# A hybrid decoder block in fp32: finer loads in the prologue, later spreading products, and three S5 inputs on GpSimd's DMA queue

## The chip, the cores and the metric

The kernel runs on one core of a Trainium2 chip. A core has a matrix engine (TensorE, PE in the profile; its weight loads are PEld), VectorE (DVE), ScalarE (ACT), GpSimd (POOL) and SyncE (SP), which here only issues DMAs. TensorE writes into PSUM banks, everything else works in SBUF; data comes from and goes to device memory (DRAM) by 16 DMA engines. A DMA is issued by SyncE, ScalarE or GpSimd, each with a queue of its own (q1, q10 and q0 in the profile). The metric is the time of one execution in device microseconds, as a median over runs; lower is better.

## The reference

One layer of a decoder block over 512 tokens and 16 meta tokens, width 1024, all in fp32. Cut to what matters here:

```
h    = concat(meta, x)                      # 528 x 1024
xn   = rmsnorm(h, g_mix_pre)
proj = xn @ w_in                            # q, k, v, r, a_low, u, z_gla, z_ssm
y_gla = gated linear attention(q, k, v, a_low, r) @ w_o_gla
y_ssm = glu(gelu(s5(u; a, log_step, b, c, d)) @ w_glu)
h    = h + rmsnorm((sigmoid(z_gla) * y_gla + sigmoid(z_ssm) * y_ssm) @ w_out, g)
h    = h + rmsnorm(relu(rmsnorm(h, g) @ w_ff1)**2 @ w_ff2, g)
```

The change touches the start: the norm of x, the first products xn @ w_in for the columns of u, and the loading of the S5 parameters b and c.

## The kernel before, in words

**Products in split precision.** Every fp32 operand is split into a high part (a rounding by ScalarE) and a low part (the rest, by VectorE), and a product of two is made of three matmuls: high-high, high-low, low-high (`mm3`, lines 190 to 198). A weight is taken as column tiles of 128: 1024 rows make eight row tiles of 128 (KT = 8), so a column tile is 512 KB and a product with it takes 8 x 3 matmuls. The tokens are handled in two parts, 256 and 272 wide (HALVES): x's first 256 tokens, then the other 256 with the 16 meta tokens.

**The prologue (lines 455 to 684)** starts the work on u before the norm of x is known. It takes x transposed (`xT`), scales its rows by the gain g alone, splits that (`rh`, `rl`, by `taken_raw`, lines 526 to 530) and multiplies the first five column tiles of the u weights with it ("raw products"); the missing factor, one per token, is applied when the product leaves PSUM (`u_took`). The factors come from x in its row layout: `squared` (ScalarE) sums the squares of a tile of 128 tokens, `rooted` (ScalarE and VectorE) makes the inverse root, `spread` (lines 550 to 556) turns the column of factors into rows by small matmuls against the identity, and `rows_of` copies them out of PSUM on ScalarE. Tokens 0 to 255 have spread(0), the others spread(1).

The order in the text, pinned on TensorE, VectorE and ScalarE:

- lines 603 to 609: for each row tile k, x's row tile is scaled and split, and between them the first two weights w0 and w1 are split in parts: row tiles 0-1, 2-3 and 4-7;
- lines 610 to 615: the products of w0 and w1 side by side, first for the first tokens (48 matmuls), then, after eight more `taken_raw`, for the others (48);
- lines 616 to 634: w2 is split, three x tiles are squared, the first two rooted; the raw product of w2 for the first tokens, with spread(0) put in ahead of row tile 3; then VectorE takes the two finished products out, scales x (`scaled`, four row tiles), splits w3, scales two more, roots the rest;
- lines 637 to 659: w2 for the other tokens, w3 for the first with spread(1) ahead of its row tile 3, w3, w4 and w4 for the rest, while x, now normed, is split into `xh` and `xl`;
- lines 660 on: the small weight of a_low (`wa`) is split; `low_rank` (line 698) is the first product with the normed x.

**Loads.** A few go by ScalarE's queue first. Two lists of SyncE loads follow (lines 475 to 480 and 495 to 514). In both, `behind()` ties each issue behind the one before it (`tc.issue_after`), so the order is the written one. The second list loads the rest of x transposed in two halves, a's parameters, weight 2, x in rows (four tiles and the meta tokens), weights 3 and 4, small weights, weight 5, then c in two layouts and b (`CA`, `CB`, `BA`, 512 KB each), weights 6 and 7. Weight tiles rotate through three buffers (`raw_w`, line 166), so a load from the fourth on waits until an earlier tile is split.

**GpSimd's queue** has in this stretch the load of `vecs` (line 515), the stores of the u tiles (`u_out`, line 285) and, at lines 681 to 683, a store of the norm factors to DRAM (`rsd`) and two loads of them in another layout (`s0`). Instructions that are not pinned or tied are ordered by the framework's scheduler, engine by engine.

`CA` is first read by `c_rows` (line 870), `BA` at line 932, `CB` in `Block.tables` (line 1174).

Of the kernel before, what the change touches and what calls it, by code (L numbers as in the profile page):

```python
# [19 lines left out]
KT = D // P  # L20
# [30 lines left out]
def hybrid_block(ctx: ExitStack, tc: tile.TileContext, io, out: bass.AP):  # L51
    nc = tc.nc
# [28 lines left out]
    def mk(pool, shape, dt=F32, tag=None, **kw):  # L81
        count[0] += 1
        name = f"{tag or 'x'}_{count[0]}"
        size = 1
        for n in shape[1:]:
            size *= n
        if pool not in lined or size % LINE == 0:
            return pool.tile(shape, dt, tag=tag or name, name=name, **kw)
        t = pool.tile([shape[0], -(-size // LINE) * LINE], dt, tag=tag or name, name=name, **kw)[:, :size]
        if len(shape) == 2:  # L90
            return t
        dims = " ".join("abcd"[: len(shape) - 1])
        return t.rearrange(f"p ({dims}) -> p {dims}", **dict(zip("abcd", shape[1:])))

    def f32(t):
        return t.bitcast(F32)
# [35 lines left out]
    def bank(tag="sm"):  # L132
        return mk(ps_mm if tag == "mm" else ps_sm, [P, 512], tag=tag)
# [29 lines left out]
    def split_hi(dst, src, scale=1.0):  # L163
        return S.activation(dst, src, AF.Copy, scale=scale)  # L164

    def raw_w(src):

        kt, n = src.shape[0] // P, src.shape[1]
        raw = mk(wp, [P, kt, P], tag="wraw", bufs=3)
        return nc.sync.dma_start(raw[:, :, :n], src.rearrange("(k p) n -> p k n", p=P)), raw  # L170

    def split_w_hi(raw):
        hi = mk(wp, [P, raw.shape[1], P], F32R, tag="whi", bufs=3)
        split_hi(hi, raw)
        return hi
# [6 lines left out]
    def split_w(raw):  # L182
        hi = split_w_hi(raw)
        return hi, split_w_lo(raw, hi)
# [15 lines left out]
    def feat_tile(w, xh, xl, c0, c1, ps, m=P, kt=KT, within=None):  # L200
        hi, lo = w
        return mm3(ps, lambda k: hi[:, k, :m], lambda k: lo[:, k, :m], lambda k: xh[:, k, c0:c1], lambda k: xl[:, k, c0:c1], kt, within)
# [90 lines left out]
    CA = mk(p5, [P, GRP, HG], tag="CA")  # L293
    CB = mk(p5, [P, GRP, HG], tag="CB")
    BA = mk(p5, [P, GRP, HG], tag="BA")
# [9 lines left out]
    def scratch():  # L305
        return mk(pg, [P, TT, P], tag="sc0", bufs=1)
# [154 lines left out]
    xT = mk(pxt, [P, KT, NT], tag="xT")  # L461
    rh, rl = (mk(pxt, [P, KT, LINE + SEQ], F32R, tag=t)[:, :, :NT] for t in ("rh", "rl"))
    raws, xts, loaded = [mk(wp, [P, KT, P], tag="wraw", bufs=3) for _ in range(2)], {}, None

    def behind():
        return tc.issue_after(loaded.ins) if loaded else ExitStack()

    def first_w(queue, i, k, n):
        return queue.dma_start(raws[i][:, k : k + n], w_in[k * P : (k + n) * P, C_U + i * P : C_U + (i + 1) * P].rearrange("(k p) n -> p k n", p=P))
# [2 lines left out]
    held = first_w(nc.scalar, 1, 0, 2)  # L472
    with tc.issue_after(held.ins):
        S.activation(warm, warm, AF.Sqrt)
    for i, k, n in (("x", 0, 1), ("x", 1, 1), (0, 2, 2), ("x", 2, 2), (1, 2, 2), ("x", 4, 2), (0, 4, 4), (1, 4, 4), ("x", 6, 2)):
        with behind():
            if i == "x":
                loaded = nc.sync.dma_start(xT[:, k : k + n, :256], io["x_cols0"][:, k : k + n])
            else:
                loaded = first_w(nc.sync, i, k, n)  # L480
# [7 lines left out]
    def x_load(t):  # L488
        n = NM if t == TT else P
        xt = mk(pxt, [P, D], tag="xt", bufs=5)  # L490
        xts[t] = xt, n
        return nc.sync.dma_start(xt[:n], io["meta_tokens"] if t == TT else io["x"][0, t * P : (t + 1) * P, :])

    early = []
    for kind, i in (("h", 0), ("h", 4), ("a", 0), ("u", 2), ("x", 0), ("x", 1), ("x", 2), ("x", 3), ("x", 4), ("u", 3), ("u", 4), ("w", 0), ("g", 0), ("u", 5), ("c", 0), ("u", 6), ("u", 7)):
        with behind():
            if kind == "x":
                loaded = x_load(i)
            elif kind == "h":
                loaded = nc.sync.dma_start(xT[:, i : i + 4, 256:], io["x_cols1"][:, i : i + 4])  # L500
            elif kind == "a":
                loaded = nc.sync.dma_start(ab, io["a_step"])
            elif kind == "w":
                wraw = mk(pg, [P, KT, 16], tag="waraw")
                loaded = nc.sync.dma_start(wraw, w_in[:, C_A : C_A + 16].rearrange("(k p) n -> p k n", p=P))
            elif kind == "g":
                wgu = scratch()[:96].rearrange("p a b -> p (a b)")
                loaded = nc.sync.dma_start(wgu, io["w_gates"])
            elif kind == "c":
                for dst, src in ((CA, io["c_cols"][0]), (CB, io["c_cols"][1]), (BA, io["b_cols"][0])):  # L510
                    loaded = nc.sync.dma_start(dst.rearrange("p g h -> p (g h)"), src)
            else:
                loaded, raw = raw_w(w_in[:, C_U + i * P : C_U + (i + 1) * P])
                raws.append(raw)
# [11 lines left out]
    def taken_raw(k, q):  # L526

        g, cols = g8[:, k : k + 1], slice(*HALVES[q])
        S.activation(rh[:, k, cols], xT[:, k, cols], AF.Copy, scale=g)
        V.scalar_tensor_tensor(rl[:, k, cols], xT[:, k, cols], g, f32(rh)[:, k, cols], op0=ALU.mult, op1=ALU.subtract)  # L530
# [19 lines left out]
    def spread(q):  # L550

        ps = bank()
        for j, i in enumerate(range(3 * q, 3 * q + 2) if not q else range(2, TT + 1)):
            n = xts[i][1]
            PE.matmul(ps[:, j * P : j * P + n], rs[:n, i : i + 1].to_broadcast([n, P]), ident[:n, :n], start=True, stop=True)
        return ps

    def rows_of(q, ps):
        a, b = HALVES[q]
        S.copy(rows[:, a:b], ps[:, : b - a])  # L560
        src = ps.rearrange("p (c s) -> p s c", s=T8)
        S.copy(rowp[:, :, 2 + a // T8 : 34 + a // T8], src[:, :, :32])
        if q:
            S.copy(rowp[:, :, :2], src[:, :, 32:34])
# [14 lines left out]
    def low(q, ks):  # L579
        cols, to = quarters_of(q)  # L580
        for k in ks:
            kk = slice(k, k + 2)
            V.tensor_sub(xl[:, kk, to], xT[:, kk, cols], f32(xh)[:, kk, to])

    def raw_product(w, q, ps, within=None):
        a, b = HALVES[q]
        feat_tile(w, rh, rl, a, b, ps[:, : b - a], within=within)
# [8 lines left out]
    def split_part(w, raw, kk):  # L596
        split_hi(w[0][:, kk], raw[:, kk])
        V.tensor_sub(w[1][:, kk], raw[:, kk], f32(w[0])[:, kk])
# [4 lines left out]
    for k in range(KT):  # L603
        taken_raw(k, 0)
        for w, raw in zip((w0, w1), raws):
            if k in (0, 2):
                split_part(w, raw, slice(k, k + 2))
            elif k == 4:
                split_part(w, raw, slice(k, KT))
    firsts = bank("mm"), bank()  # L610
    side_by_side((w0, w1), 0, firsts)
    for k in range(KT):
# [3 lines left out]
    w2_ = split_w(raws[2])  # L616
# [5 lines left out]
    work(1.3)  # L622
    squared(2)
    pair2, spreads = bank("mm"), []
    raw_product(w2_, 0, pair2, (3, lambda: spreads.append(spread(0))))
    rows_of(0, spreads[0])
    for i in range(2):
        u_took(firsts[i][:, :256], uts[i], 0, True)
# [2 lines left out]
    w3 = split_w(raws[3])  # L631
# [5 lines left out]
    last[2] = bank()  # L637
    raw_product(w2_, 1, last[2])
    low(0, (0, 2))
    raw_product(w3, 0, pair2[:, 256:], (3, lambda: spreads.append(spread(1))))  # L640
    w4_hi = split_w_hi(raws[4])
    high(0, range(4, 8))
    rows_of(1, spreads[1])
# [37 lines left out]
    nc.gpsimd.dma_start(rsd.rearrange("(t p) -> p t", p=P), rs[:, :TT])  # L681
    for i in range(2):
        nc.gpsimd.dma_start(s0[i * CH : (i + 1) * CH], rsd.rearrange("(c t i) -> i c t", t=TT, i=2)[i])
    sx.close()

    sga = ExitStack()
# [137 lines left out]
    with tc.issue_after(loaded.ins):  # L824
        loaded = nc.sync.dma_start(bn, io["b_rows"])
# [925 lines left out]
    loaded = nc.gpsimd.dma_start(gpost, io["g_mix_post"][0].partition_broadcast(P))  # L1751
# [356 lines left out]
```

## Time and profile before

| | us |
|---|---|
| median of 3 runs | 858.37 |
| lowest and highest | 857.73, 859.96 |
| the profiled execution | 858.26 |
| its span, first to last instruction | 856.5 |
| TensorE busy in the span | 846.2 (99%) |
| VectorE busy | 687.5 (80%) |
| ScalarE busy | 465.4 (54%) |
| GpSimd busy | 150.9 (18%) |

A timeline row reads: start in us, length in us, engine, line, operation, output <- inputs, shape, count, and in brackets how long the engine was idle before it and what ended that. Line 61 is the helper that issues every matmul, line 79 the one that issues the pinned VectorE and ScalarE instructions, so the operands tell what a row is. The lengths of matmuls are modelled and overlap; their starts tell the pace. DMA issue rows give the time on the issuing queue, not the transfer. A row of windows gives, for a stretch, each engine's busy time, the granted TensorE clock (1.00 is full), the DMA engines' mean share and GB/s.

### The profile page before, as it was taken

What the parts mean: (1) busy time and instruction counts of PE and PEld (TensorE: products, weight loads), DVE (VectorE), ACT (ScalarE), POOL (GpSimd) and SP (SyncE); (2) the same over time, 40 slices, a digit from 0 to 9 for tenths busy, and PEclk for the clock granted to TensorE, in tenths of its full rate; (3) what the DMA queues carried; (4) which work ended last, traced back from release to release, by engine and by line L of the source; (5) the groups of instructions that cost most, each with busy time, mean ns of one, the idle gap of its engine ahead of it and who ended that gap; (6) DMA issues with size and microseconds to landing.
All of it is one profiled execution on the core that took longest, in us unless ns stands there. A gap on an engine that the chain in (4) does not pass through costs nothing.

```text
span 856.5 us, 13814 instructions
## 1 busy us (share of the span) xinstructions
PE 846.2 (99%) x4974; PEld 725.7 (85%) x4974; DVE 687.5 (80%) x1282; ACT 465.4 (54%) x824; POOL 150.9 (18%) x265
## 2 busy tenths in 40 slices
PE   9999999999999999999999999999999999999996
PEld 8998989898988888888888889888888888888884
DVE  6999889998989599855888687667666777688886
ACT  7677465866855545433545465333222246885762
POOL 1223120240313123241211421011111100000000
PEclk9999999999999999999999999999999999999999
DMA  9887766576465868686898896498989967766564
GB/s 311 200 280 226 224 145 155 136 178 175 124 168 152 234 177 164 215 269 198 243 284 260 278 288 211 135 332 287 345 284 330 362 219 244 256 197 198 175 202 138
DMA packets 172492, 192.67 MB, mean 225 GB/s; under 512 B 18648, under 2 KB 127720, under 8 KB 172424
## 3 DMA queue, kind: packets, MB, share of 16 engines
q1 hardware_dynamic: 145040, 109.66, 44.9%
q0 software_dynamic: 25408, 77.93, 27.3%
q10 hardware_dynamic: 1976, 4.20, 1.6%
q8 instruction: 39, 0.64, 0.3%
q14 instruction: 29, 0.24, 0.1%
HBM read 149.52 MB, written 42.24 MB: 224 GB/s over the span
## 4 chain that ended last, share of the span: by engine, by line
PE 89%; DVE 6%; DMA 2%; issue 1%; ACT 1%; DVEq 0%; ACTq 0%; SPq 0%
PE mm L61 69%; PE sm L61 19%; PE sm L66 2%; DMA wraw<-in_w_in_dram 1%; DMA wraw<-t2d 1%; DVE wlo L1946 1%; DVE wlo L179 1%; DVE c L2028 0%; DMA U<-ud 0%; DVE rs L1311 0%; DVE c L2003 0%; DVE ogl L1313 0%; DVE xT L79 0%; ACT whi L1942 0%; DVE rs L1310 0%
## 5 line engine op out<-in xcount | busy, mean ns | idle before, releaser
L164 ACT ACTIVATE whi<-wraw 128x1024 fp32r<-128x1024 f32 x81 | 85.9, 1060 | 176.0 <-PE mm L61 167.2
L61 PE MATMUL mm<-xh,whi 128*128 128x512 f32 (+2 forms) x464 | 157.4, 339 | 0.0
L61 PE MATMUL mm<-xh,wlo 128*128 128x512 f32 (+2 forms) x464 | 155.2, 335 | 0.0
L61 PE MATMUL mm<-xl,whi 128*128 128x512 f32 (+2 forms) x464 | 155.1, 334 | 0.0
L179 DVE TENSOR_TENSOR wlo<-wraw,whi 128x1024 fp32r<-128x1024 f32 x81 | 98.6, 1219 | 69.8 <-ACT whi L164 69.8
L61 PE MATMUL mm<-hh,whi 128*128 128x512 f32 (+2 forms) x272 | 100.7, 370 | 0.0
L61 PE MATMUL mm<-hh,wlo 128*128 128x512 f32 (+2 forms) x272 | 100.6, 370 | 0.0
L61 PE MATMUL mm<-hl,whi 128*128 128x512 f32 (+2 forms) x272 | 100.6, 370 | 0.0
L61 PEld LDWEIGHTS mm<-xh,wlo 128*128 128x128 f32 x464 | 87.3, 188 | 8.9
L61 PEld LDWEIGHTS mm<-xh,whi 128*128 128x128 f32 x464 | 87.2, 188 | 8.8 <-issue 0.3
L61 PEld LDWEIGHTS mm<-xl,whi 128*128 128x128 f32 x464 | 87.3, 188 | 8.5
L1946 DVE TENSOR_TENSOR wlo<-wraw,whi 128x1024 fp32r<-128x1024 f32 x56 | 68.4, 1223 | 23.9 <-ACT whi L1942 23.8
L61 PE MATMUL sm<-wlo,fh 128*128 128x512 f32 x192 | 74.9, 390 | 0.4 <-DVE wlo L1946 0.4
L61 PE MATMUL sm<-whi,fl 128*128 128x512 f32 x192 | 74.7, 389 | 0.0
L61 PE MATMUL sm<-whi,fh 128*128 128x512 f32 x192 | 74.7, 389 | 0.0
L1942 ACT ACTIVATE whi<-wraw 128x1024 fp32r<-128x1024 f32 x56 | 58.6, 1049 | 18.7 <-PE mm L61 11.7
L61 PEld LDWEIGHTS mm<-hh,whi 128*128 128x128 f32 x272 | 51.1, 188 | 8.8
L61 PEld LDWEIGHTS mm<-hl,whi 128*128 128x128 f32 x272 | 51.1, 188 | 8.7
L61 PEld LDWEIGHTS mm<-hh,wlo 128*128 128x128 f32 x272 | 51.1, 188 | 8.7
L61 PE MATMUL mm<-gh,whi 128*128 128x512 f32 x128 | 49.8, 389 | 0.0
L61 PE MATMUL mm<-gl,whi 128*128 128x512 f32 x128 | 49.8, 389 | 0.0
L61 PE MATMUL mm<-gh,wlo 128*128 128x512 f32 x128 | 49.8, 389 | 0.0
(535 smaller groups left out, 1858.4 us busy)
## 6 DMA issues: line engine op xcount, KB each, us to landing
wraw<-in_w_ff_dram SPq DMA_DIRECT2D x56, 512.0 KB
wraw<-in_w_in_dram SPq DMA_DIRECT2D x46, 512.0 KB
w2raw<-in_w_ff_dram POOLq DMA_DIRECT2D x16, 1024.0 KB, 8.7
t2d<-w2t POOLq DMA_DIRECT2D x16, 1024.0 KB, 6.1
wraw<-t2d SPq DMA_DIRECT2D x32, 512.0 KB
wraw<-in_w_glu_dram SPq DMA_DIRECT2D x16, 512.0 KB
M<-kpad POOLq DMA_DIRECT2D x64, 64.0 KB, 3.0
wraw<-in_w_o_gla_dram SPq DMA_DIRECT2D x8, 512.0 KB
```

What stands on the lines that cost most here:

```text
L61: ins = nc.tensor.matmul(*args, **kw)
L66: ins = nc.tensor.transpose(*args, **kw)
L164: return S.activation(dst, src, AF.Copy, scale=scale)
L179: V.tensor_sub(lo, raw, f32(hi))
L1942: halved = S.activation(bh, raw, AF.Copy)
L1946: V.tensor_sub(bl, raw, f32(bh))
```

## The change

In the first list of loads the second halves of w0 and w1 come in quarters with x's last part between them; x's first half of the remaining tokens comes in two pieces; the split of w0 and w1 follows in four parts instead of three. Both spreading products stand ahead of row tile 7 instead of 3. The three loads of c and b leave SyncE's second list and stand behind the loads of `s0`, issued by GpSimd, without a tie to another instruction.

```diff
@@ -472,7 +472,7 @@
-    for i, k, n in (("x", 0, 1), ("x", 1, 1), (0, 2, 2), ("x", 2, 2), (1, 2, 2), ("x", 4, 2), (0, 4, 4), (1, 4, 4), ("x", 6, 2)):
+    for i, k, n in (("x", 0, 1), ("x", 1, 1), (0, 2, 2), ("x", 2, 2), (1, 2, 2), ("x", 4, 2), (0, 4, 2), (1, 4, 2), ("x", 6, 2), (0, 6, 2), (1, 6, 2)):
@@ -492,12 +492,12 @@
-    for kind, i in (("h", 0), ("h", 4), ("a", 0), ("u", 2), ("x", 0), ("x", 1), ("x", 2), ("x", 3), ("x", 4), ("u", 3), ("u", 4), ("w", 0), ("g", 0), ("u", 5), ("c", 0), ("u", 6), ("u", 7)):
+    for kind, i in (("h", (0, 2)), ("h", (2, 4)), ("h", (4, 8)), ("a", 0), ("u", 2), ("x", 0), ("x", 1), ("x", 2), ("x", 3), ("x", 4), ("u", 3), ("u", 4), ("w", 0), ("g", 0), ("u", 5), ("u", 6), ("u", 7)):
...
-                loaded = nc.sync.dma_start(xT[:, i : i + 4, 256:], io["x_cols1"][:, i : i + 4])
+                loaded = nc.sync.dma_start(xT[:, slice(*i), 256:], io["x_cols1"][:, slice(*i)])
@@ -506,9 +506,6 @@
-            elif kind == "c":
-                for dst, src in ((CA, io["c_cols"][0]), (CB, io["c_cols"][1]), (BA, io["b_cols"][0])):
-                    loaded = nc.sync.dma_start(dst.rearrange("p g h -> p (g h)"), src)
@@ -603,10 +600,8 @@
-            if k in (0, 2):
+            if k % 2 == 0:
                 split_part(w, raw, slice(k, k + 2))
-            elif k == 4:
-                split_part(w, raw, slice(k, KT))
@@ -622,7 +617,7 @@
-    raw_product(w2_, 0, pair2, (3, lambda: spreads.append(spread(0))))
+    raw_product(w2_, 0, pair2, (7, lambda: spreads.append(spread(0))))
@@ -637,7 +632,7 @@
-    raw_product(w3, 0, pair2[:, 256:], (3, lambda: spreads.append(spread(1))))
+    raw_product(w3, 0, pair2[:, 256:], (7, lambda: spreads.append(spread(1))))
@@ -681,6 +676,8 @@
     for i in range(2):
         nc.gpsimd.dma_start(s0[i * CH : (i + 1) * CH], rsd.rearrange("(c t i) -> i c t", t=TT, i=2)[i])
+    for dst, src in ((CA, io["c_cols"][0]), (CB, io["c_cols"][1]), (BA, io["b_cols"][0])):
+        nc.gpsimd.dma_start(dst.rearrange("p g h -> p (g h)"), src)
     sx.close()
```

## The prediction

> **What bounds the kernel now.** I read the page first, then the chain of work that ended last, then each engine's timeline of the first 50 us, then the DMA queues.
>
> ```profile
> span 856.5 us, 13814 instructions
> PE 846.2 (99%) x4974; PEld 725.7 (85%) x4974; DVE 687.5 (80%) x1282; ACT 465.4 (54%) x824; POOL 150.9 (18%) x265
> ```
>
> TensorE sets the time nearly everywhere. The profiled execution took 858.26 us, 1.8 more than its span and 0.1 under the median 858.37. The change touches only the first 45 us, so I follow the chain there.
>
> ```profile
> 4.90 4.39 DMA wraw<-in_w_in_dram
> ...
> 20.32 0.46 PE sm L61 x4
> ...
> 23.82 1.14 DVE wlo L79
> ...
> 26.63 1.00 PE sm L61 x6
> ...
> 38.28 9.52 PE mm L61 x80
> ```
>
> Columns: start, length, what. The chain runs from the load of w1's second half (landed 4.90 + 4.39 = 9.3) through its split to TensorE, through both products of w0 and w1 to the first spreading product (spread(0)), over to VectorE (scaled rows of x, the low part of w3 at 23.82), through the second root to spread(1), and from there stays on TensorE. Whatever delays spread(0) delays everything behind it.
>
> **Part 1, smaller loads.** TensorE in the first product:
>
> ```profile
> 9.39 0.28 PE L61 MATMUL mm<-rl,whi 128*128 128x256 f32 x1
> 9.71 0.38 PE L61 MATMUL mm<-rh,wlo 128*128 128x256 f32 x1
> ...
> 10.73 0.39 PE L61 MATMUL sm<-rh,wlo 128*128 128x256 f32 x1 [0.23 <-DVE wlo L79]
> ...
> 11.47 0.28 PE L61 MATMUL sm<-rh,whi 128*128 128x256 f32 x1
> ...
> 13.17 0.28 PE L61 MATMUL mm<-rh,whi 128*128 128x272 f32 x1
> ```
>
> Fifteen matmuls lie between 11.47 and 13.17, so the free pace is 1.70 / 15 = 0.113 us. From 9.39 to 11.47 there are 8 steps, worth 0.9 us at that pace; they took 2.08. So 1.17 us are lost to w1's second half. With quarters, rows 4-5 of w0 and w1 come before the last quarter of x, and their splits are half as long. Rows 6-7 of w1 come after that quarter (256 KB, 0.78 us at the 335 GB/s quoted below), at 9.3 + 0.8 = 10.1 instead of 9.3, and are needed twelve matmuls (1.4 us) later than rows 4. I estimate 0.2 us of stall left and a gain of 1.0: the next product (13.17) starts at 12.2. What is late next there is x's other half:
>
> ```profile
> 11.69 3.42 ACT L79 ACTIVATE rh<-xT,g 128x272 fp32r<-128x272 f32 x8 [0.54 <-DMA xT<-in_x_cols_dram]
> ```
>
> Its first eighths waited for DMA until 11.69; cut in (0,2), (2,4), (4,8) the first piece comes about 0.7 us earlier, which fits the earlier start. ScalarE and VectorE get four smaller splits instead of two, SyncE three more issues; SyncE issues far ahead of the transfers, so they cost nothing while that backlog lasts, and some 0.4 us each without it.
>
> **Part 2, spreading products.**
>
> ```profile
> 16.21 1.06 ACT L79 ACTIVATE xt<-xt 128x1024 f32<-128x1024 f32 x1 [0.16 <-DMA xt<-in_x_dram]
> 19.53 0.16 DVE L79 SCALAR_TENSOR_TENSOR xrs<-xra,xrs 128x2 f32<-128x2 f32 x1
> 20.15 0.61 PE L61 MATMUL sm<-ident,xrs 128*128 128x128 f32 x4
> 25.51 0.28 PE L61 MATMUL mm<-rh,wlo 128*128 128x256 f32 x1
> 26.22 0.28 PE L61 MATMUL mm<-rh,wlo 128*128 128x256 f32 x1
> ```
>
> The first root is ready at 19.69 and spread(0) starts at 20.15, without a wait. One microsecond earlier it would wait half a microsecond; twelve matmuls later (1.4 us) it starts at 20.15 - 1.0 + 1.4 = 20.55. TensorE gains, but the row scales that VectorE waits for come 0.4 us later than now. VectorE works without idling behind them, so w3's low part, ready now at 24.96, comes at 25.35, against the first matmul that needs it, now at 25.51. TensorE is then held there and has gained only 0.15. Spread(1) stops waiting (26.34 to 26.63): 0.3 more. Parts 1 and 2 alone: -0.45 us, 857.8; bounds 0 (the 0.4 grows) and -1.0 (the whole first gain survives). Behind spread(1) the low-rank product at 38.28 has 1.3 us of slack to its last input (0.28 long, below).
>
> ```profile
> 36.66 0.28 DVE L79 TENSOR_TENSOR wa<-waraw,wa 128x128 fp32r<-128x128 f32 x1
> ```
>
> **Part 3, the S5 inputs: where they land in GpSimd's queue.** They leave an ordered list (each load issued after the one before) and stand, with no input and nothing holding them, behind the loads of s0. How such instructions are placed shows in GpSimd's timeline:
>
> ```profile
> 2.64 0.71 POOL L515 DMA_DIRECT2D vecs<-in_vecs_dram  x1
> 26.80 0.79 POOL L681 DMA_DIRECT2D rsd<-xrs  x1 [23.44 <-DVE xrs L79]
> 38.40 1.24 POOL L683 DMA_DIRECT2D vecs<-rsd  x2 [10.82 <-DMA rsd<-xrs]
> ...
> 45.15 0.55 POOL L948 MEMSET sc<- 128x512 f32 x1
> 48.52 0.55 POOL L286 DMA_DIRECT2D ud<-ut  x1 [2.82 <-ACT ut L79]
> ```
>
> The memset of line 948 stands in the program behind all eight early slots, yet runs before the store of the first of them (L286 at 48.52): order on this engine goes by readiness, unless it is pinned. The loads of CA, CB and BA write fresh tiles and read kernel inputs; they are ready from the start, and GpSimd is empty from 3.35 to 26.8. I expect them right behind vecs, at 3.4 to 5.0 us, not behind s0 (L683, done at 39.64). That puts three loads of 512 KB into the stretch that is full:
>
> ```profile
> 5.00:10.00 5.00, 4.95 (x30) 4.42 (x28) 3.88 (x10) 4.27 (x11) 0.00 (x0) 1.00 1.08 335
> ...
> 15.00:20.00 5.00, 5.00 (x43) 5.00 (x42) 3.67 (x15) 4.69 (x9) 0.00 (x0) 1.00 1.04 387
> ...
> CA<-in_c_cols_dram SPq DMA_DIRECT2D x1, 512.0 KB
> ...
> BA<-in_b_cols_dram SPq DMA_DIRECT2D x1, 512.0 KB
> ```
>
> The last two columns are the DMA engines' busy share (over 1: full) and GB/s. 1.573 MB in long rows move at between 387 (the x tiles, in the second row) and 427 GB/s (below): 3.7 to 4.1 us, I take 3.9. How GpSimd's queue (q0) fares beside SyncE's (q1) when both have work, the windows 43 to 46 and 44 to 45 show:
>
> ```profile
> q0 software_dynamic: 316, 1.01, 85.0%
> q1 hardware_dynamic: 313, 0.15, 18.6%
> ...
> DMA packets 128, 0.43 MB, mean 427 GB/s; under 512 B 27, under 2 KB 27, under 8 KB 128
> ```
>
> Long rows on q0 moved 1.01 MB while the 512 B rows on q1 moved 0.15. So q1 nearly stands still while the S5 inputs pass, and all that lands later comes 3.9 us later. [...]
>
> Splits of two rows now:
>
> ```profile
> 5.64 0.42 ACT L79 ACTIVATE whi<-wraw 128x256 fp32r<-128x256 f32 x1 [0.31 <-DMA wraw<-in_w_in_dram]
> 6.09 0.42 DVE L79 TENSOR_TENSOR wlo<-wraw,whi 128x256 fp32r<-128x256 f32 x1 [0.31 <-ACT whi L79]
> ```
>
> The sum: w1's last rows land at 10.1 + 3.9 = 14.0; split high and low (0.42 each), one more row of x's low part (0.43, an eighth of 3.42) and five matmuls (0.6) bring the first product's end to 15.9, against 13.17. From there to spread(0) is 20.15 - 13.17 + 1.4 = 8.4: 24.3. The roots hang on the x tiles: 19.69 + 3.9 = 23.6. So spread(0) starts between 23.6 and 24.3, 3.45 to 4.15 later than now; take 3.8. From that come off 0.55 (slack at 25.51) and 0.3 (spread(1)'s wait): +2.95, bounds +2.6 and +3.3. A delay on the chain passes to the end in full. 858.26 + 2.95 = 861.2; on the scale of the median 861.3. On SyncE the three issues go, but the next load there (w6) waits for w3's buffer, free at 24.96, anyway; w6 and w7 then land sooner, which delays nobody and is worth nothing as long as the chain above sets the time.
>
> **Rivals.** A: the S5 loads keep their written place, at about 39.6. For it: they are written behind the s0 loads; against it: the memset row. Their first reader comes late:
>
> ```profile
> L79 ACT ACTIVATE CA<-CA,sgn x1: 1158/1158/1158, 75.3 to 75.3; 128x1024 f32<-128x1024 f32 x1
> ```
>
> Three issues of some 0.55 us push back the stores of ud queued behind them by 1.7 us, and the total is that of parts 1 and 2, 857.8: not slower.
>
> B: they go early, but q0 gets few turns. For it:
>
> ```profile
> rsd<-xrs POOLq DMA_DIRECT2D x1, 2.0 KB, 11.3
> ```
>
> Two kilobytes on q0 took 11.3 us to land while q1 was full; but those are 4 B elements, not 4 KB rows. Then q1 loses less than half of the 3.4 us between A and the forecast: from -0.45 to +1.25, in the middle 858.7.
>
> C: TensorE falls back to its slow pace. It starts at 0.21 us a matmul:
>
> ```profile
> 7.03 0.41 PE L61 MATMUL mm<-rh,whi 128*128 128x256 f32 x1
> 7.25 0.36 PE L61 MATMUL mm<-rl,whi 128*128 128x256 f32 x1
> ```
>
> With the loads held up, TensorE stands for 2 to 2.5 us before row 4 and about 1 before row 6. If that returns it to 0.22 for 6 us, 27 matmuls instead of 54 are done, 3 us more: 864.2. Against it: half-microsecond gaps at 9.4 to 10.7 did not. [...]
>
> **How the numbers follow.** Forecast 0.68, A 0.15, B 0.10, C 0.07. About 0.3% (2.6 us) is what a measurement of this kernel can tell from no change. The forecast lies at that edge: of its 0.68 I give 0.49 to over 0.3%, since its whole band from +2.6 up is there and only an error of mine takes it below; with C, slower 0.56. A, B and the rest make 0.42 within; faster by that much needs more than all the stalls of part 1 and 2: 0.02. Range 857.4 to 863.0: from A's better half over B and the forecast (860.9 to 861.6 by its bounds, widened for the landing times that I read only by who waited for them); left out is C and a little of A. The forecast's own range is 860.0 to 862.8.
>
> **What would show it.** GpSimd's timeline: three DMA issues of the S5 inputs near 3.4 to 5 us (right), or near 40 (A). Queue q0 with about 1.5 MB between 5 and 11 us, q1 nearly still. Spread(0) near 24, the square of the first x tile near 20 instead of 16.21, the low-rank product near 41. If the S5 inputs come early and the first square is still at 16 to 17, q0 gave way (B). If spread(0) starts at 20.5 and the time falls by over 1 us, my holding point at w3's low part is wrong.

## The result, and the profile after

The changed kernel takes 863.22 us (median of 5 runs, 863.03 to 864.08), the kernel before beside it 858.63 (5 runs, 857.73 to 859.96): 1.0054 times as long, 95% interval 1.0044 to 1.0065. It is slower by 4.6 us. The prediction had 861.3 with a range up to 863.0, so the result lies outside it: the direction and the main cause were right, the size was too small by 1.9. Of that, 0.26 is the kernel before itself, 858.63 over these five runs and 858.37 over the three that the prediction had.

The page of the changed kernel, whose profiled execution took 863.03 us:

```profile
span 861.3 us, 13826 instructions
PE 847.3 (98%) x4974; PEld 726.8 (84%) x4974; DVE 688.0 (80%) x1284; ACT 466.2 (54%) x826; POOL 153.0 (18%) x268
```

TensorE has as many matmuls as before and 1.1 us more of busy time in a span 4.8 us longer. So most of the loss is TensorE standing. GpSimd's timeline of the changed kernel:

```profile
2.65 0.71 POOL L512 DMA_DIRECT2D vecs<-in_vecs_dram  x1
3.36 0.55 POOL L680 DMA_DIRECT2D CA<-in_c_cols_dram  x1
3.89 0.55 POOL L680 DMA_DIRECT2D CB<-in_c_cols_dram  x1
4.42 0.55 POOL L680 DMA_DIRECT2D BA<-in_b_cols_dram  x1
```

The S5 loads are issued right behind vecs, as forecast, not near 40 us. The DMA queues of the changed kernel from 5 to 11 us (packets, MB, share of 16 engines):

```profile
q0 software_dynamic: 437, 1.53, 65.5%
q1 hardware_dynamic: 1059, 0.72, 38.0%
```

Queue q0 moved 1.53 MB there, the three S5 inputs; the queue of the weights and of x got 0.72 MB, and from 8 to 11 us only 0.19 against 1.00. ScalarE's timeline of the changed kernel shows what came late by it:

```profile
12.04 0.72 ACT L79 ACTIVATE whi<-wraw 128x256 fp32r<-128x256 f32 x2 [1.98 <-DMA wraw<-in_w_in_dram]
...
13.47 0.71 ACT L79 ACTIVATE whi<-wraw 128x256 fp32r<-128x256 f32 x2
...
19.64 1.06 ACT L79 ACTIVATE xt<-xt 128x1024 f32<-128x1024 f32 x1 [0.26 <-DMA xt<-in_x_dram]
```

Rows 4-5 of w0 and w1 are split at 12.04, rows 6-7 at 13.47, and the first x tile is squared at 19.64 (16.21 before). TensorE's timeline of the changed kernel:

```profile
9.13 0.28 PE L61 MATMUL sm<-rh,wlo 128*128 128x256 f32 x1
12.51 0.58 PE L61 MATMUL mm<-rh,whi 128*128 128x256 f32 x1 [3.10 <-ACT whi L79]
...
16.90 0.28 PE L61 MATMUL mm<-rh,whi 128*128 128x272 f32 x1
...
25.30 0.61 PE L61 MATMUL sm<-ident,xrs 128*128 128x128 f32 x4
...
30.15 0.38 PE L61 MATMUL mm<-rh,wlo 128*128 128x256 f32 x1 [0.70 <-DVE wlo L79]
...
42.50 0.28 PE L61 MATMUL mm<-xh,wa 128*32 128x256 f32 x1
```

Between 9.13 and 12.51 TensorE stands for the weight rows. The next product (16.90) is 3.7 us later than before, spread(0) (25.30) 5.15, the low-rank product (42.50) 4.38. The low-rank product of the kernel before is this row of its timeline; the 38.28 of the prediction and of the first expectation is where the piece of the chain begins that it opens:

```profile
38.12 0.28 PE L61 MATMUL mm<-xh,wa 128*32 128x256 f32 x1
```
The windows of the changed kernel around the gap; the third number from the right is the granted clock:

```profile
9.00:12.00 3.00, 0.41 (x4) 0.20 (x2) 0.48 (x1) 0.51 (x1) 0.00 (x0) 1.00 1.05 387
12.00:13.00 1.00, 0.49 (x2) 0.49 (x3) 0.51 (x2) 0.96 (x3) 0.00 (x0) 0.70 1.13 358
13.00:15.00 2.00, 2.00 (x11) 2.00 (x11) 2.00 (x6) 2.00 (x7) 0.00 (x0) 0.50 1.08 386
15.00:16.00 1.00, 1.00 (x8) 1.00 (x7) 1.00 (x4) 1.00 (x3) 0.00 (x0) 0.59 1.08 379
```

At the end of the gap the clock falls to 0.50, and the ten matmuls from 13.35 on, up to 15.48, follow each other at 0.21 us instead of the 0.113 of the kernel before. That is rival C's mechanism, smaller than it was priced.

My theory after the result: the S5 bytes that run ahead of the weights make a gap, and the gap costs twice, by its length and by a slow clock behind it. Rivals: the smaller loads or the later spreading products cost the time; the clock costs nothing because TensorE waits for rows anyway; the early position alone does not matter.

### The profile page after: what moved, and what is told of

The parts are those of the page before. It is cut to its first block, busy times and chain, and to the rows that moved or that the text cites. A ratio compares the mean times of both kernels' runs of the same rounds, so it can differ in the third digit from the quotient of the medians.

```text
span 861.3 us, 13826 instructions
## 1 busy us (share of the span) xinstructions
PE 847.3 (98%) x4974; PEld 726.8 (84%) x4974; DVE 688.0 (80%) x1284; ACT 466.2 (54%) x826; POOL 153.0 (18%) x268
## 4 chain that ended last, share of the span: by engine, by line
PE 91%; DVE 5%; DMA 2%; issue 1%; ACT 1%; SPq 0%; DVEq 0%
PE mm L61 68%; PE sm L61 21%; PE sm L66 2%; DMA wraw<-in_w_in_dram 1%; DVE wlo L179 1%; DMA ro<-og 1%; DVE rs L1308 0%; DMA g<-in_g_cols_dram 0%; DVE ogl L1310 0%; DVE c L2025 0%; DVE rs L1307 0%; DVE xT L79 0%; DVE c L2000 0%; DVE qt L1277 0%; DVE v L1250 0%
```

## The experiments

All ratios are against the kernel before, run on the same chip (medians 858.3 to 858.6). Stage times are the starts, in us, of the first matmul of each stage in the one profiled execution; kernels whose prologue loads are the same differ there by up to 0.35 (next product 12.53 to 12.88 with part 1 alone, with parts 1 and 2, and with the S5 loads tied).

| kernel | median us (runs) | ratio, 95% interval | next product | spread(0) | low-rank |
|---|---|---|---|---|---|
| before | 858.63 (5) | | 13.17 | 20.15 | 38.12 |
| changed | 863.22 (5) | 1.0054 (1.0044 to 1.0065) | 16.90 | 25.30 | 42.50 |
| parts 1 + 2 | 859.01 (10) | 1.0002 (0.9993 to 1.0012) | 12.88 | 21.41 | 38.67 |
| part 3 alone | 863.30 (4) | 1.0056 (1.0041 to 1.0071) | 18.75 | 25.73 | 43.70 |
| part 1 alone | 859.00 (10) | 1.0007 (0.9998 to 1.0017) | 12.75 | 20.63 | 38.70 |
| part 2 alone | 859.07 (10) | 1.0010 (1.0000 to 1.0019) | 13.33 | 21.73 | 38.99 |
| parts 1 + 2, one S5 load early | 859.60 (10) | 1.0016 (1.0007 to 1.0026) | 13.57 | 21.97 | 39.16 |
| parts 1 + 2, two early | 862.10 (4) | 1.0044 (1.0029 to 1.0059) | 16.17 | 24.90 | 42.08 |
| the same, gap filled | 861.06 (9) | 1.0028 (1.0018 to 1.0038) | 15.74 | 24.14 | 41.34 |
| changed, gap filled | 862.50 (4) | 1.0041 (1.0026 to 1.0056) | 17.00 | 25.40 | 42.60 |
| parts 1 + 3 | 862.61 (4) | 1.0050 (1.0035 to 1.0065) | 18.30 | 25.56 | 43.55 |
| changed, S5 loads tied behind s0 | 860.65 (10) | 1.0024 (1.0014 to 1.0033) | 12.53 | 21.33 | 38.52 |
| part 1, a_step after two x tiles | 858.73 (10) | 1.0000 (0.9990 to 1.0009) | 12.51 | 19.84 | 38.67 |
| part 1, a_step on GpSimd's queue | 858.74 (11) | 1.0002 (0.9993 to 1.0011) | 12.24 | 19.63 | 38.02 |

**Which part.** Parts 1 and 2 with the S5 loads back in SyncE's list:

```diff
-("u", 5), ("u", 6), ("u", 7)
+("u", 5), ("c", 0), ("u", 6), ("u", 7)
...
+            elif kind == "c":
+                for dst, src in ((CA, ...), (CB, ...), (BA, ...)):
+                    loaded = nc.sync.dma_start(dst.rearrange("p g h -> p (g h)"), src)
...
-    for dst, src in ((CA, ...), (CB, ...), (BA, ...)):
-        nc.gpsimd.dma_start(dst.rearrange("p g h -> p (g h)"), src)
```

> The changed kernel with the S5 inputs put back at their old place in SyncE's list: parts 1 and 2 alone. Theory L (the S5 inputs going early on GpSimd's queue cost everything, through late loads and a TensorE that fell to its slow pace): no gap over 0.6 us in the first product, the next product starts at 12.0 to 12.4, spread(0) at 20.4 to 20.7, the low-rank product at 37.5 to 38.1 instead of 38.28, total 0.2 to 0.8 us under the kernel before. Rival S (spreading four row tiles later is what delays VectorE): spread(0) is late here as well and the total is 1 us or more above the kernel before.

And the kernel before with nothing but the S5 loads moved, by the same two edits the other way round:

> The kernel before with part 3 alone: coarse loads, spreading products at row tile 3, S5 inputs early on GpSimd's queue. Theory L: the first product stands 3 to 4.5 us before row tile 4, then goes at 0.21 us a matmul for about 3 us; next product at 17.5 to 18.5, spread(0) at 24.5 to 25.5, total 4.3 to 5.5 us above the kernel before. Rival S: the delay needs the later spreading products, total at most 3 us above the kernel before.

Measured: 859.01 and 863.30. Part 3 alone makes the whole loss (its next product and spread(0) come a quarter of a microsecond past the bounds expected); parts 1 and 2 leave the time where it was, where 0.2 to 0.8 under the kernel before was expected. In the profile parts 1 and 2 bring the next product only 0.3 earlier and the low-rank product 0.55 later, so together they did not gain what the forecast took. They were then tried one by one. Part 1 alone is the first kernel with the spreading products at row tile 3 again; part 2 alone is one number in two lines of the kernel before:

```diff
-    raw_product(w2_, 0, pair2, (3, lambda: ...
+    raw_product(w2_, 0, pair2, (7, lambda: ...
-    raw_product(w3, 0, pair2[:, 256:], (3, lambda: ...
+    raw_product(w3, 0, pair2[:, 256:], (7, lambda: ...
```

> The kernel before with part 1 alone: spreading products behind row tile 3, S5 loads in SyncE's list. The prediction's step would give a next product at 12.2, spread(0) at 19.7 (held by the root), and 0.4 us off the time. My theory now: SyncE's three more issues push the x tiles back by 0.9, so the first root is ready at 20.66 instead of 19.69 and spread(0) waits for it until 21.0 to 21.1, later than 20.15; w3's low part then comes 0.9 later than now, less 0.55 of slack: low-rank product at 38.3 to 38.6, time 858.5 to 858.9, no gain.

> The kernel before with part 2 alone: both spreading products behind row tile 7. Theory: spread(0) at 21.5 instead of 20.15, VectorE's rows 1.4 later, w3's low part at 26.3 instead of 24.96, TensorE held there for 0.8, and 0.3 given back at spread(1): low-rank product at 38.6 instead of 38.12, time 858.9. Rival (the prediction's step taken by itself: spread(1)'s wait goes and the delay at w3 is covered by the slack of 0.55): low-rank at 37.8 to 38.1, time 858.1 to 858.4.

Part 1 alone: low-rank at 38.70, within 0.1 of the theory's range, and no gain. The late root was right, but the number was hit by luck: spread(0) came at 20.63, not 21.0 to 21.1, and no wait for w3's low part follows; TensorE simply carries the 0.48 by which spread(0) is late, and 0.1 more, to the low-rank product. TensorE's timeline of part 1 alone shows the wait for the root:

```profile
20.63 0.68 PE L61 MATMUL sm<-ident,xrs 128*128 128x128 f32 x4 [0.74 <-DVE t L79]
```

Part 2 alone: low-rank at 38.99, 0.39 past the expected 38.6, of which 0.16 is a next product that started later (13.33). TensorE's timeline of part 2 alone at w3's low part:

```profile
26.58 0.38 PE L61 MATMUL mm<-rh,wlo 128*128 128x256 f32 x1 [0.69 <-DVE wlo L79]
```

From the next product to the low-rank product the kernel before and part 3 alone take 24.95 us, both with spreading products at row tile 3; the changed kernel takes 25.60 and part 2 alone 25.66. So where no root is late the later position costs 0.65 to 0.7 us of TensorE's time and gains nothing, though the interval of the whole kernel for it reaches down to no change. Where spread(0) waits for the root anyway it costs nothing more: low-rank at 38.67 with parts 1 and 2, 38.70 with part 1 alone.

**How much of it is bytes.** Parts 1 and 2, with one or two of the three S5 loads on GpSimd's queue and the others in SyncE's list (the diff is of one early, against parts 1 and 2; for two, CB follows CA):

```diff
-                for dst, src in ((CA, ...), (CB, ...), (BA, ...)):
+                for dst, src in ((CB, ...), (BA, ...)):
...
+    nc.gpsimd.dma_start(CA.rearrange("p g h -> p (g h)"), io["c_cols"][0])
```

> The kernel with parts 1 and 2 alone (859.01, next product at 12.88), and of the three S5 loads only CA on GpSimd's queue, free to run early; CB and BA stay in SyncE's list. With three early the next product starts at 16.90, 4.02 later. Theory T1 (bytes alone set the delay, the slow matmuls after the gap cost nothing, since TensorE waits for the next row anyway): 1.34 us for each load, so the next product at 14.2, the time 860.3. Theory T2 (2.8 us of the 4.02 are bytes, 0.94 for each load, and 1.2 the 15 matmuls at 0.21 us, which come only with the long gap): the next product at 13.8, the pace behind the gap 0.113, the time 859.9. Rival T3 (what is early costs nothing until it makes a gap of 3 us): 12.9 and 859.0.

> As with one early, but CA and CB on GpSimd's queue and BA alone in SyncE's list. T1: the next product at 15.55, the time 861.7. T2: the next product at 14.75, a gap of some 2 us, the pace behind it 0.113, the time 860.9. T3: 12.9 to 13.5, 859.0 to 859.6. If matmuls at 0.21 us show behind a gap shorter than 3 us, the slow pace comes with less idle time than the 3.38 us seen in the changed kernel.

With one early, 13.57 and 859.60: nearest to T2, a little cheaper. With two early, T2's 14.75 failed: 16.17, and 862.10 against its 860.9. The windows of that kernel say why:

```profile
11.00:12.00 1.00, 0.40 (x2) 0.30 (x2) 0.77 (x3) 0.87 (x3) 0.00 (x0) 1.00 1.12 362
...
13.00:14.00 1.00, 1.00 (x7) 1.00 (x8) 1.00 (x4) 1.00 (x4) 0.00 (x0) 0.73 1.07 387
14.00:15.00 1.00, 1.00 (x7) 1.00 (x6) 1.00 (x3) 1.00 (x4) 0.00 (x0) 0.50 1.08 372
15.00:16.00 1.00, 1.00 (x7) 1.00 (x7) 0.98 (x3) 0.55 (x3) 0.00 (x0) 0.50 1.16 362
16.00:17.00 1.00, 1.00 (x7) 1.00 (x6) 0.55 (x2) 1.00 (x3) 0.00 (x0) 0.56 1.12 400
```

The gap was 2.56 us from start to start (9.04 to 11.60), shorter than T2 allowed for, and the clock still fell, nearly two microseconds after TensorE had begun again. T2's split into bytes and clock stands, its condition (only a gap of over 3 us) does not.

**Is the clock worth time?** Matmuls of ones with ones into an unused bank, ahead of row tile 4, keep TensorE busy in the gap; nothing reads them. Seven in the changed kernel, then five in the kernel with two loads early:

```diff
         for k in range(KT):
+            if q == 0 and k == 4:
+                busy(7)
             for (hi, lo), ps in zip(ws, pss):
```

> The changed kernel with seven dummy matmuls (ones by ones, 256 wide, into the idle bank) ahead of row tile 4 of the first product, so that TensorE is not idle while the loads are late. Theory C (the 3.4 us gap returned TensorE to its slow pace, which cost 1.5 us on top of the late loads): after row tile 4 the matmuls go at 0.113 us, the next product starts near 15.6 instead of 17.07, spread(0) near 23.8 instead of 25.3, total 1.2 to 1.6 us under the changed kernel, some 3.1 above the kernel before. Rival D (the loads alone set the end of the first product): next product still at 16.8 to 17.1, total within 0.3 us of the changed kernel.

> The kernel with two S5 loads early, and five matmuls of ones with ones into an unused bank ahead of row tile 4 of the first product (2.3 us, in the gap of 2.56 us; nothing reads them). Theory: the clock of 0.50 that TensorE was granted from 13.4 to 16.9 us comes from the idle gap; with the gap filled it stays at 1.00, the matmuls stay at 0.113 us, the next product starts at about 14.9 instead of 16.17, and the time is 860.9 to 861.1 against 862.1. Rival: the loads set the end of the first product, the slow clock costs next to nothing: 16.0 and 862.0.

With the gap filled the clock stays at 1.00 in both. The windows of the kernel with two loads early and the gap filled:

```profile
13.00:14.00 1.00, 1.00 (x8) 0.89 (x9) 1.00 (x4) 1.00 (x5) 0.00 (x0) 1.00 1.09 391
14.00:15.00 1.00, 1.00 (x11) 1.00 (x10) 1.00 (x4) 1.00 (x4) 0.00 (x0) 1.00 1.08 370
```

The median fell from 862.10 to 861.06, as expected, and in the changed kernel from 863.22 to 862.50, by 0.7 and not by the 1.2 to 1.6 expected; in both pairs the intervals overlap, so the totals alone do not settle it. The start of the next product does not either: at 15.74 and 17.00 it missed the theory's 14.9 and 15.6, and 17.00 is what rival D had. In these two profiles the last weight rows are split 0.7 and 1.1 us later than without the filling. With two loads early the delay is there from w1's first rows on (the first matmul with them at 6.72, behind a wait of 0.58 for their split, against 6.38), ahead of the filling; in the changed kernel most of it comes later, and why stays open. What settles it is the stretch that landing times drop out of, from the split of the last weight rows (6-7) to the next product. ScalarE's and TensorE's timelines of parts 1 and 2 show its two ends, the first row of the table:

```profile
10.42 0.80 ACT L79 ACTIVATE whi<-wraw 128x256 fp32r<-128x256 f32 x2
...
12.88 0.28 PE L61 MATMUL mm<-rh,whi 128*128 128x272 f32 x1
```

| kernel | split of rows 6-7 | next product | between | lowest clock |
|---|---|---|---|---|
| parts 1 + 2 | 10.42 | 12.88 | 2.46 | 1.00 |
| part 1 alone | 10.29 | 12.75 | 2.46 | (0.12 us a matmul) |
| one early | 11.07 | 13.57 | 2.50 | 1.00 |
| two early, gap filled | 13.32 | 15.74 | 2.42 | 1.00 |
| changed, gap filled | 14.53 | 17.00 | 2.47 | 1.00 |
| two early | 12.64 | 16.17 | 3.53 | 0.50 |
| changed | 13.47 | 16.90 | 3.43 | 0.50 |
| parts 1 + 3 | 13.94 | 18.30 | 4.36 | 0.50 |

At full clock (for part 1 alone judged by the pace from 12.28 to 12.75) it is 2.42 to 2.50, with the slow clock 1.0 or 1.9 more. So the clock costs the changed kernel 0.97 us at this place, and the bytes the rest: rows 6-7 split at 13.47 instead of 10.42, 3.05.

Parts 1 and 3 without part 2 were meant to show part 2's cost a second time:

> The changed kernel with both spreading products back behind row tile 3 (parts 1 and 3 alone). Theory: the root is ready at 23.13 there, so spread(0) starts at 23.9 instead of 25.30, w3's low part comes 1.4 earlier, and TensorE, held at it from 29.18 to 30.15, gains that 0.97, less 0.3 for a wait before spread(1): low-rank product at 41.8 instead of 42.50, time 862.5. Rival (the position of the spreading products costs nothing): low-rank at 42.5, time 863.2.

Low-rank came at 43.55, not 41.8, and 862.61 is within the interval of the changed kernel: as a test of part 2 in the total it is inconclusive. The windows of this kernel show what covered it:

```profile
12.00:13.00 1.00, 0.02 (x1) 0.02 (x1) 0.04 (x1) 0.49 (x2) 0.00 (x0) 0.53 1.13 363
...
18.00:19.00 1.00, 1.00 (x7) 1.00 (x6) 1.00 (x4) 1.00 (x4) 0.00 (x0) 0.56 1.07 427
```

In this execution the clock stayed low from about 12.1 to 18.9, twice as long as in the changed kernel, and the next product came 1.4 us later (0.47 of it because rows 6-7 are split later). From there to the low-rank product it took 25.25, of which some 0.3 are the last slow matmuls: 24.95 again, as in the kernel before and with part 3 alone.

**The written place.** The S5 loads tied behind the loads of s0, so that they run near 39 us, rival A's case:

```diff
+    with tc.issue_after(last_s0.ins):
         for dst, src in ((CA, ...), (CB, ...), (BA, ...)):
             nc.gpsimd.dma_start(dst.rearrange("p g h -> p (g h)"), src)
```

> The changed kernel with the three S5 loads tied behind the s0 loads on GpSimd, so that they go where they are written (near 40 us). Theory L: the first 39 us as with the loads back on SyncE (spread(0) at 20.4 to 20.7, the low-rank product at 37.5 to 38.1), total 0.2 to 0.8 us under the kernel before; q0 carries 1.5 MB between 41 and 47 us and nothing on TensorE waits for it. Rival Q (GpSimd's queue is the wrong one at any place): waits on TensorE between 42 and 60 us, total above the kernel before.

The start is that of parts 1 and 2 (low-rank 38.52), yet the kernel takes 860.65, 1.6 more than those (the intervals just part). The theory had it 0.2 to 0.8 under the kernel before; it is 2.2 above. Rival Q's waits on TensorE between 42 and 60 us do not show either. The loss comes behind 40 us, by a longer way. SyncE's issue of the next load (bn) with the S5 loads tied:

```profile
43.47 9.12 SPq L823 DMA_DIRECT2D bn<-in_b_rows_dram  x1
```

With parts 1 and 2 alone the same issue took 1.61 us (at 43.55). The weight behind it is late, and so is its split on ScalarE, in the timeline of the tied kernel:

```profile
55.69 1.06 ACT L79 ACTIVATE whi<-wraw 128x1024 fp32r<-128x1024 f32 x1 [3.34 <-DMA wraw<-in_w_in_dram]
```

It stands at 51.59 with parts 1 and 2 alone. VectorE idles for 3.94 us there, falls behind, and TensorE pays some twenty microseconds later; TensorE's waits in the tied kernel from 64 to 100 us (in total, times, longest):

```profile
PE mm L61 <- DVE wlo L79: 2.7, 3, 1.0
```

The kernel with parts 1 and 2 has no such wait. That the tied loads cause it follows from the one edit between the two; why bn's issue took 9.12 us stays open (from 43 to 53 us q1 moved 0.83 MB against 1.86 with parts 1 and 2, and q0 2.84 against 1.89).

**Why part 1 gained so little.** Windows 8 to 10 us with parts 1 and 2; the last two columns are the DMA engines' share and GB/s:

```profile
8.00:9.00 1.00, 1.00 (x10) 0.98 (x10) 1.00 (x4) 1.00 (x4) 0.00 (x0) 1.00 0.94 194
9.00:10.00 1.00, 1.00 (x11) 1.00 (x10) 0.89 (x3) 0.35 (x2) 0.00 (x0) 1.00 0.87 203
```

The kernel before:

```profile
8.00:9.00 1.00, 1.00 (x11) 1.00 (x10) 0.87 (x4) 0.90 (x2) 0.00 (x0) 1.00 1.01 331
9.00:10.00 1.00, 0.95 (x7) 0.65 (x6) 0.67 (x2) 0.68 (x2) 0.00 (x0) 1.00 1.03 323
```

SyncE's issues of the x tiles, in the kernel before and with parts 1 and 2:

```profile
8.80 3.44 SPq L492 DMA_DIRECT2D xt<-in_x_dram  x4
...
9.92 3.39 SPq L492 DMA_DIRECT2D xt<-in_x_dram  x4
```

The suspicion: with three issues more, SyncE's issuing is the limit. The issue of a_step took it 0.84 us in the kernel before and 0.75 with parts 1 and 2, so that load was first moved behind two x tiles, and then taken off SyncE altogether, both in part 1 alone:

```diff
-("h", (4, 8)), ("a", 0), ("u", 2), ("x", 0), ("x", 1), ("x", 2)
+("h", (4, 8)), ("u", 2), ("x", 0), ("x", 1), ("a", 0), ("x", 2)
```

> Part 1 alone, with the load of a_step (0.75 to 0.84 us of SyncE's time to issue, first read at 17.6) moved behind the first two x tiles. Theory: SyncE's issuing is what makes the x tiles late once there are three loads more, so the first square comes at 16.2 instead of 17.00, the first root at 19.6, spread(0) no longer waits (19.8 instead of 20.63), low-rank product at 37.9 instead of 38.70, time 858.2 against 859.0. Rival (the bytes, not the issues, make them late): first square at 17.0, nothing changes.

```diff
-("h", (4, 8)), ("a", 0), ("u", 2)
+("h", (4, 8)), ("u", 2)
...
+    nc.gpsimd.dma_start(ab, io["a_step"])
```

> Part 1 alone, with the load of a_step (98 KB) given to GpSimd's queue, so that SyncE issues it no more and the x tiles go out 0.8 us earlier. Theory (issuing is what part 1 lacks): all five x tiles earlier than in part 1 alone, the third square no longer waiting for its load (it waited until 20.25 with a_step between the second and third tile), spread(0) at 19.8 without a wait, the second root at 26.4, low-rank product at 37.9 against 38.70 with part 1 alone and 38.12 before; time 858.2, equal to the kernel before or 0.2 under it. Rival (bytes, not issues, make the x tiles late, or a_step's bytes on GpSimd's queue hold the weight rows up): low-rank at 38.6 or later, time 859.0.

Behind two x tiles: the first square at 16.17 and spread(0) at 19.84, as expected (though spread(0) still waits a little for the root), but the low-rank product at 38.67, not 37.9. ScalarE's timeline of that kernel shows the third x tile paying instead:

```profile
20.25 1.06 ACT L79 ACTIVATE xt<-xt 128x1024 f32<-128x1024 f32 x1 [1.35 <-DMA xt<-in_x_dram]
```

On GpSimd's queue: the next product at 12.24, which is the prediction's 12.2; first square at 16.00, third without a wait, low-rank at 38.02 (37.9 expected). Windows 8 to 10 us of that kernel:

```profile
8.00:9.00 1.00, 1.00 (x10) 0.99 (x10) 1.00 (x4) 1.00 (x4) 0.00 (x0) 1.00 1.01 311
9.00:10.00 1.00, 1.00 (x10) 1.00 (x10) 0.81 (x4) 0.79 (x3) 0.00 (x0) 1.00 1.06 345
```

With parts 1 and 2, whose two lists of loads are those of part 1 alone, the same two windows have 194 and 203 GB/s (above), so with one issue less on SyncE the loads flow again. The x tiles are issued 1.06 earlier than there (8.86 instead of 9.92), and the first square comes 1.00 earlier than with part 1 alone (16.00 instead of 17.00). The 96 KB that leave the queue with the issue are worth 0.28 us at 345 GB/s, an estimate from the row above. So it was the issues more than the bytes that made part 1 late. The time is that of the kernel before (858.74; 1.0002, 0.9993 to 1.0011), and no version tried here beats it. Where the 0.93 gained at the next product goes, TensorE's timeline of this kernel shows: spread(0) now waits for its root, and spread(1) longer than before for its own.

```profile
19.63 0.68 PE L61 MATMUL sm<-ident,xrs 128*128 128x128 f32 x4 [0.25 <-DVE t L79]
...
26.54 0.68 PE L61 MATMUL sm<-ident,xrs 128*128 128x128 f32 x4 [0.44 <-DVE xrs L79]
```

From the next product to spread(0) it takes 0.41 more than before, from there to spread(1) 0.43 more, which leaves 0.1. Part 2 together with this placing of a_step was not tried.

## Why the prediction was right in direction and short in size

- **S5 loads run early: right**, issued at 3.36 to 4.97 us, with 1.53 MB on q0 from 5 to 11. Rivals A and B fell.
- **All that lands later comes 3.9 us later: somewhat too much.** Against parts 1 and 2 alone, rows 4-5 are split 3.87 later in the changed kernel (12.04 against 8.17), rows 6-7 3.05, and its first x tile is squared 2.46 later (19.64 against 17.18); for the last two it is 4.1 and 3.7 in its version with the gap filled.
- **First product's end at 15.9: the step that failed.** The slow clock behind the gap was put at nothing in the sum and cost 0.97. The other two terms cancel, by luck: counted from the first of the two splits of rows 6-7 (13.47), the start at 14.0 was 0.53 too late, and splits and matmuls, put at 1.9, take 2.46 at full clock (0.56 more); counted from w1's own split (13.8), which the sum starts with, both are off by some 0.2. Sum: +1.0, and 16.90 it was. Rival C was set aside, at 0.07, on steps of half a microsecond that had not slowed TensorE (clock 1.00 from 9 to 11 us in the kernel before). The gap was 3.38, not 2 to 2.5, and the kernel with two loads early shows that 2.56 is enough. C's price of 3 us was too high as well: the slow stretch lasts 3.42 us, not the 6 it was given, and costs 0.97. The range left C out, and so its upper end of 863.0 lay under the result.
- **From there to spread(0) 8.4: right** (25.30 - 16.90 = 8.40). Spread(0) waited for TensorE's arrival, not for the root, ready at 23.13. The prediction took the middle between the two, 3.8, instead of its own later end, 4.15: 0.35 lost.
- **0.55 and 0.3 come off behind spread(0): right**, 5.15 - 4.38 = 0.77, with TensorE held at w3's low part (30.15). These recover part of what the later position cost, they are no gain.
- The three items (1.0, 0.35, 0.08) make 1.43 at the low-rank product: 4.38 against 2.95. The other 0.42 of the span's 4.8 arises later; from the low-rank product to the end of the span it takes 818.80 against 818.38, and 817.8 to 819.7 in the experiments other than the tied one, so it is within what executions differ by.
- **Parts 1 and 2 alone at -0.45: wrong**, +0.55 at the low-rank product, and the total unchanged within its interval. The step that failed is part 1's: the next product at 12.88, not 12.2, because of "SyncE issues far ahead of the transfers, so they cost nothing while that backlog lasts". With three issues more the backlog did not last (194 and 203 GB/s from 8 to 10 us), and the second price given there, 0.4 us each, fits the 1.12 by which the x tiles were issued later. Spread(0) then starts at 21.41, 0.86 behind the 20.55 forecast; the rest of part 2's working held, down to the wait at w3's low part (0.85 forecast, 0.97 - 0.12 = 0.85 measured with parts 1 and 2 alone, 25.29 to 26.26).
- **Rival A costless: wrong**, had it come true; the tied kernel loses 1.6 us against parts 1 and 2.

## What to carry to other kernels

A load that waits for nothing went to the front of an idle queue here, whatever line it was written on. Ask what it passes: 1.5 MB ahead of the first weights cost more here than anything that the finer loads could give, and tied to its line it hurt a later stage instead. When a forecast makes the matrix engine stand for some 2.5 us or more (2.56 was the shortest gap here that slowed the clock), price the slow clock behind the gap as a term of the sum, by the length of the slow stretch and not by the gap (0.50 for some 3.42 us in three kernels here, 6.82 in a fourth). And count issues as well as bytes: in this prologue, with pieces of 128 KB, the issuing engine was the limit (194 and 203 GB/s from 8 to 10 us with three issues more, 311 and 345 in part 1 alone with the issue of a_step taken off SyncE).

## What the runs showed of the hardware

- The granted clock fell to 0.50 with gaps of 2.56, 3.38 and 3.83 us from one matmul's start to the next's (two early, changed, and both kernels with 3.83: parts 1 + 3 and part 3 alone); idle for 2.29, 3.10 and some 3.55 us of that, TensorE slowed, and idle for up to 0.89 (changed, gap filled) and 1.0 (the tied kernel's waits between 64 and 100 us, with the clock at 1.00 from 40 to 80 and from 80 to 200) it did not. By the averages of the windows, taken as steps between 1.00 and 0.50, the clock stayed low for an estimated 3.42 us (two early: 0.54 + 2 + 0.88), 3.42 (changed: 0.60 + 2 + 0.82), 3.42 (part 3 alone: 0.08 + 3 + 0.34) and 6.82 (parts 1 + 3), one or two times the same length; which of the two it is does not follow from the gap, since the two kernels with 3.83 differ. With two loads early it fell at about 13.46, 1.9 us after TensorE had begun again, with part 3 alone at about 14.92, 1.6 us after. Idle times between 1.0 and 2.29 us were not tried.
- Two queues with work did not share evenly: in the changed kernel, from 8 to 11 us, the 4 KB rows on q0 moved 1.00 MB in 274 packets while the weights and x on q1 moved 0.19 in 356.
